# SwiGLU gate and up with the weights stationary and both parts of the tokens streaming, in a four-FFN decoder trunk

## The chip, the cores and the metric

The kernel runs on one core of one Trainium2 chip. The core has a matrix engine (TensorE, PE in the profile), a vector engine (VectorE, DVE), a scalar engine (ScalarE, ACT), a general engine (GpSimd, POOL) and a queue engine that issues DMAs (SyncE, SP). Work lives in SBUF, matmul results in PSUM, which has eight banks of 128 partitions x 512 fp32 columns. The metric is the device time of one execution in microseconds; the median of 3 runs of the kernel before is 1009.85 us (1009.16 to 1009.86).

## The reference, cut to what matters

256 tokens of 1024 channels pass through two layers. In each layer, an FFN, a mixer and another FFN are added to the residual x, so there are four FFNs:

```python
for layer in range(2):
    x = x + 0.5 * swiglu(rms_norm(x, norm_ffn1[layer]), w_ffn1_in[layer], w_ffn1_out[layer])
    x = x + mixer(rms_norm(x, norm_mix[layer]))      # layer 0: convolution and sparse attention, layer 1: stick-breaking
    x = x + 0.5 * swiglu(rms_norm(x, norm_ffn2[layer]), w_ffn2_in[layer], w_ffn2_out[layer])
return rms_norm(x, norm_final)

def swiglu(x, w_in, w_out):                          # w_in 1024 x 5632, w_out 2816 x 1024
    gate, up = jnp.split(x @ w_in, 2, axis=-1)
    return (jax.nn.silu(gate) * up) @ w_out
```

All of it is float32. The norm divides each token by its own root mean square; its gain is per channel.

## The kernel before, in words

Every large product is made of three matmuls on split operands. A weight block arrives by DMA in a raw tile of 1 MB (SP's queue, line 74), ScalarE copies it to a rounded high part `wh` (L84) and VectorE takes the difference as a low part `wl` (L85); activations are split likewise into XH and XL. `mm3` (L202 to L204) then adds high x high, high x low and low x high in one PSUM bank.

Before an FFN the residual x [tokens, channels] is turned to channels on partitions. For each half t of the tokens and half hf of the channels, four transposes on TensorE (L143) write one bank, and ScalarE (L156) and VectorE (L157) evacuate it in four steps as XH and XL, each step taking its turn on the same tile. The gain goes in there. The norm factor of a token is not known yet at that point; squares on ScalarE (L126) and two small steps on GpSimd (L130, L131) make it, and it is applied later.

Gate and up: the tokens are stationary (128 of them at a time) and the weights stream, 512 columns wide (256 of gate and 256 of up). A chunk of 256 channels takes 2 halves of tokens x 8 channel blocks x 3 matmuls, and there are 11 chunks. The result has tokens on partitions, so the norm factor is a scalar per partition: SiLU (L226) and the product (L228) take it along. For the output product the result must have channels on partitions, so `act_turn` turns it: two transposes on TensorE (L235), a copy on ScalarE (L239), a subtraction on VectorE (L240). The output product `out_mm` of a chunk is issued one chunk later, into four banks that stay open through the FFN. At the end the residual is updated (L300) tile by tile, and the next stage's transposes wait in a list that `flush` issues.

PSUM: two banks for gate and up (ps_gu), two for transposes (ps_tr), four for the output (ps_po). In the first chunk of an FFN t=0 goes first as a whole, so that the transposes of t=1 stand in its middle. In the others the halves alternate.

The order on each engine is made by a scheduler when the program is built, from the order in which instructions are written and their dependences; each engine then runs its own list in order and waits on semaphores. `begin` fixes the order of the first chunk by hand: it fetches x in four pieces and the first weights in eight pieces of 256 KB, runs nine matmuls on zeros while they arrive, and turns half of the channels at a time.

Of the kernel before, what the change touches and what calls it, by code (L numbers as in the profile page):

```python
# [8 lines left out]
F32 = mybir.dt.float32  # L9
# [7 lines left out]
P = 128  # L17
# [4 lines left out]
NCH = 11  # L22
# [24 lines left out]
def trunk_kernel(ctx: ExitStack, tc: tile.TileContext, a: dict):  # L47
# [46 lines left out]
    nc.sync.dma_start(gains, a["gains"])  # L94
# [5 lines left out]
    gfin = [None]  # L100
    XH = [None]
    XL = [None]
    RS = [None]

    def new_xt():
        XH[0] = acts.tile([P, ND, T], F32R, tag="XH", name="XH")
        XL[0] = acts.tile([P, ND, T], F32R, tag="XL", name="XL")
# [3 lines left out]
    half = const.tile([P, 1], F32, name="half")  # L111
    G.memset(half, -0.5)
# [15 lines left out]
    def rms(t):  # L128
        ms = small.tile([P, 1], F32, tag="ms", name="ms")
        G.tensor_scalar(ms, sq[t][:, 0:1], sq[t][:, 1:2], EPS, op0=ALU.add, op1=ALU.add)  # L130
        latest["pool"] = G.tensor_tensor(RS[0][:, t:t + 1], ms, half, op=ALU.pow)  # L131
# [8 lines left out]
    def turn_pe(src):  # L140
        pt = bank(ps_tr, "tr")
# [4 lines left out]
    def turn(t, hf, src, ni):  # L146

        pt = turn_pe(src)
        evacuate(pt, t, hf, ni, range(4))

    def evacuate(pt, t, hf, ni, ks):
        for k in ks:
            dt = hf * 4 + k
            g = gains[:, ni, dt:dt + 1]
            ts = slice(t * P, (t + 1) * P)
            latest["act"] = S.activation(XH[0][:, dt, ts], pt[:, k * P:(k + 1) * P], AF.Copy, scale=g)  # L156
            latest["dve"] = V.scalar_tensor_tensor(XL[0][:, dt, ts], pt[:, k * P:(k + 1) * P], g, f(XH[0][:, dt, ts]),  # L157
                                                   op0=ALU.mult, op1=ALU.subtract)
# [3 lines left out]
    def flush():  # L162
        for go in pending:
            go()
        pending.clear()

    def updated(t, hf, then):
# [5 lines left out]
        if kind == "ffn":  # L173
            pending.append(lambda: turn(t, hf, halves(t, hf), ni))
# [14 lines left out]
        if kind == "mix":  # L189
            for h in range(2):  # L190
                hs = slice(h * 512, (h + 1) * 512)
                V.tensor_scalar(o[:, hs], halves(t, h), r, None, op0=ALU.mult)
                pending.append(lambda h=h, hs=hs: turn(t, h, o[:, hs], ni))
# [18 lines left out]
    def ffn(w_in, w_out, then, first=None):  # L212
        xh, xl, rs = XH[0], XL[0], RS[0]
        po = {}
        hT = {}

        def gu_mm(pg, t, dt, w):
            (wh, wl), o = w[dt // 2], (dt % 2) * 512
            ts = slice(t * P, (t + 1) * P)
            mm3(pg, xh[:, dt, ts], xl[:, dt, ts], wh[:, o:o + 512], wl[:, o:o + 512], dt == 0, dt == ND - 1)  # L220

        hs = {}

        def act(t, pg):
            sg = small.tile([P, T], F32, tag="sg", name="sg", bufs=2)
            latest["silu"] = S.activation(sg, pg[:, :T], AF.Silu, scale=rs[:, t:t + 1])  # L226
            h = small.tile([P, T], F32, tag="h", name="h", bufs=2)
            V.scalar_tensor_tensor(h, pg[:, T:], rs[:, t:t + 1], sg, op0=ALU.mult, op1=ALU.mult)  # L228
            hs[t] = h

        def act_turn(c, t):
            h = hs[t]
            pt = bank(ps_tr, "tr")
            for k in range(2):
                PE.transpose(pt[:, k * P:(k + 1) * P], h[:, k * P:(k + 1) * P], ident)  # L235
            hh = small.tile([P, 2, P], F32R, tag="hh", name="hh", bufs=6)
            hl = small.tile([P, 2, P], F32R, tag="hl", name="hl", bufs=6)
            pv = pt[:, :T].rearrange("p (k q) -> p k q", k=2)
            S.activation(hh, pv, AF.Copy)  # L239
            V.tensor_tensor(hl, pv, f(hh), op=ALU.subtract)  # L240
            hT[c, t] = hh, hl

# [728 lines left out]
```

## Time and profile before

| | before |
|---|---|
| median of 3 runs | 1009.85 us |
| profiled execution | 1010.14 us |
| its span | 1008.4 us |
| PE busy | 992.9 us (98%), 5048 matmuls |
| PE weight loads busy | 825.3 us (82%) |
| DVE busy | 598.7 us (59%) |
| ACT busy | 542.2 us (54%) |
| DMA, mean share of 16 engines | 49% |
| HBM traffic | 175.9 MB, 174 GB/s |
| mean granted PE clock | 0.999 |

The span is that of the core's instructions; 1.7 us of the profiled execution lie around it. The profile names an instruction by its line in the kernel's file, its engine and its tiles (out <- in). Busy time of PE is the sum over time in which at least one matmul is in flight, so it says little about how closely they follow each other; the distance from start to start does.

### The profile page before, as it was taken

How to read it: one execution, taken by the hardware profiler on the slowest of the kernel's cores; microseconds unless marked ns; L12 is line 12 of the kernel's file. 1: busy time of each engine (PE TensorE's matmuls, PEld its weight loads, DVE VectorE, ACT ScalarE, POOL GpSimd, SP SyncE). 2: the span in 40 equal slices, each digit the busy share in tenths (PEclk: the TensorE clock that was granted, in tenths of full speed). 3: DMA queues.
4: the chain of work that ended last, by engine and by line, in shares of the span. 5: the costliest groups of instructions: out<-in, count | busy, mean ns of one | idle time of the engine just before them, and what ended most of it. 6: DMA issues, size and time to landing. Idle time of an engine off the chain costs nothing.

```text
span 1008.4 us, 13048 instructions
## 1 busy us (share of the span) xinstructions
PE 992.9 (98%) x5048; PEld 825.3 (82%) x5048; DVE 598.7 (59%) x891; ACT 542.2 (54%) x944; POOL 51.5 (5%) x97
## 2 busy tenths in 40 slices
PE   8999999999999999999999999999999999999997
PEld 6888888788888888888878888887898788888885
DVE  5655555599855655555575555546777575555553
ACT  7544444587545544444474444445887474444443
POOL 4000000132111000000000000000000010000001
PEclk9999999999999999999999999999999999999999
DMA  8745454454433654545445454553632255554521
GB/s 319 271 170 205 170 206 135 146 194 161 164 126 110 228 205 169 206 170 204 168 168 201 175 200 175 198 177 125 247 118 98 84 205 210 172 204 172 204 105 42
DMA packets 26702, 176.72 MB, mean 175 GB/s; under 512 B 3344, under 2 KB 3472, under 8 KB 5904
## 3 DMA queue, kind: packets, MB, share of 16 engines
q1 hardware_dynamic: 26640, 175.89, 49.1%
q8 instruction: 39, 0.64, 0.3%
q14 instruction: 23, 0.19, 0.1%
HBM read 174.83 MB, written 1.05 MB: 174 GB/s over the span
## 4 chain that ended last, share of the span: by engine, by line
PE 74%; issue 18%; DVE 3%; ACT 2%; POOL 1%; DMA 1%; SPq 0%; POOLq 0%; ACTq 0%
PE gu L203 11%; PE gu L202 11%; PE gu L204 11%; PE po L202 8%; PE po L203 8%; PE po L204 8%; PE gu L353 3%; PE gu L355 3%; PE gu L354 3%; PE tr L235 1%; PE tr L143 1%; ACT wh L84 1%; DVE wl L85 1%; DMA raw<-in_w_in 1%; PE po L787 1%
## 5 line engine op out<-in xcount | busy, mean ns | idle before, releaser
L85 DVE TENSOR_TENSOR wl<-raw,wh 128x1024 fp32r<-128x1024 f32 (+3 forms) x388 | 397.2, 1038 | 295.1 <-ACT wh L84 293.8
L84 ACT ACTIVATE wh<-raw 128x1024 fp32r<-128x1024 f32 (+3 forms) x396 | 349.3, 899 | 317.0 <-PE gu L204 169.3
L202 PE MATMUL gu<-wh,XH 128*128 128x512 f32 (+1 forms) x688 | 267.6, 389 | 1.4 <-ACT XH L156 1.3
L204 PE MATMUL gu<-wh,XL 128*128 128x512 f32 (+1 forms) x688 | 266.9, 388 | 0.1
L203 PE MATMUL gu<-wl,XH 128*128 128x512 f32 (+1 forms) x688 | 266.6, 387 | 0.0
L202 PEld LDWEIGHTS gu<-wh,XH 128*128 128x128 f32 x688 | 129.1, 188 | 29.7 <-ACT XH L156 3.8
L204 PEld LDWEIGHTS gu<-wh,XL 128*128 128x128 f32 x688 | 129.1, 188 | 26.8 <-DVE XL L157 0.6
L203 PEld LDWEIGHTS gu<-wl,XH 128*128 128x128 f32 x688 | 129.2, 188 | 26.6 <-DVE wl L85 0.4
L202 PE MATMUL po<-wh,hh 128*128 128x512 f32 x352 | 143.9, 409 | 0.0
L204 PE MATMUL po<-wh,hl 128*128 128x512 f32 x352 | 138.0, 392 | 0.0
L203 PE MATMUL po<-wl,hh 128*128 128x512 f32 x352 | 137.8, 392 | 0.0
L353 PE MATMUL gu<-XH,wh 128*128 128x256 f32 x288 | 83.7, 291 | 1.6 <-DVE u L476 1.2
L355 PE MATMUL gu<-XH,wl 128*128 128x256 f32 x288 | 81.4, 283 | 0.0
L354 PE MATMUL gu<-XL,wh 128*128 128x256 f32 x288 | 81.4, 283 | 0.0
L204 PEld LDWEIGHTS po<-wh,hl 128*128 128x128 f32 x352 | 66.1, 188 | 14.1
L203 PEld LDWEIGHTS po<-wl,hh 128*128 128x128 f32 x352 | 66.4, 189 | 11.5
L202 PEld LDWEIGHTS po<-wh,hh 128*128 128x128 f32 x352 | 66.2, 188 | 11.3
L226 ACT ACTIVATE sg<-gu,rs 128x256 f32<-128x256 f32 x80 | 38.0, 475 | 61.3 <-PE gu L204 61.2
L353 PEld LDWEIGHTS gu<-XH,wh 128*128 128x128 f32 x288 | 55.1, 191 | 2.0 <-issue 1.3
L228 DVE SCALAR_TENSOR_TENSOR h<-gu,rs,sg 128x256 f32<-128x256 f32 x80 | 38.7, 483 | 30.2 <-ACT sg L226 30.2
L354 PEld LDWEIGHTS gu<-XL,wh 128*128 128x128 f32 x288 | 55.1, 191 | 0.1
L355 PEld LDWEIGHTS gu<-XH,wl 128*128 128x128 f32 x288 | 55.0, 191 | 0.0
(207 smaller groups left out, 874.5 us busy)
## 6 DMA issues: line engine op xcount, KB each, us to landing
raw<-in_w_in SPq DMA_DIRECT2D x86, 1024.0 KB, 4.7
raw<-in_w_out SPq DMA_DIRECT2D x44, 1024.0 KB, 4.7
raw<-in_w_ab SPq DMA_DIRECT2D x10, 1024.0 KB, 4.8
raw<-in_w_qk SPq DMA_DIRECT2D x8, 1024.0 KB, 4.8
raw<-in_w_out_ab SPq DMA_DIRECT2D x4, 1024.0 KB, 4.7
raw<-in_w_v SPq DMA_DIRECT2D x4, 1024.0 KB, 4.7
raw<-in_w_out_sb SPq DMA_DIRECT2D x4, 1024.0 KB, 4.9
raw<-in_w_in SPq DMA_DIRECT2D x8, 256.0 KB, 6.3
```

Source lines behind the costliest of these rows:

```text
L84: S.activation(h[:, ms], r[:, ms], AF.Copy)
L85: eng.tensor_tensor(l[:, ms], r[:, ms], f(h[:, ms]), op=ALU.subtract)
L143: PE.transpose(pt[:, k * P:(k + 1) * P], src[:, k * P:(k + 1) * P], ident)
L202: PE.matmul(out, lh, rh, start=first, stop=False)
L203: PE.matmul(out, lh, rl, start=False, stop=False)
L204: PE.matmul(out, ll, rh, start=False, stop=last)
L226: latest["silu"] = S.activation(sg, pg[:, :T], AF.Silu, scale=rs[:, t:t + 1])
L228: V.scalar_tensor_tensor(h, pg[:, T:], rs[:, t:t + 1], sg, op0=ALU.mult, op1=ALU.mult)
L235: PE.transpose(pt[:, k * P:(k + 1) * P], h[:, k * P:(k + 1) * P], ident)
L353: PE.matmul(pq, wh[:, dt], XH[0][:, dt], start=dt == 0, stop=False)
L354: PE.matmul(pq, wh[:, dt], XL[0][:, dt], start=False, stop=False)
L355: PE.matmul(pq, wl[:, dt], XH[0][:, dt], start=False, stop=dt == ND - 1)
```

## The change

Gate and up are computed with the weights stationary: a block of 128 columns of gate or of up is loaded, and the tokens stream. XH and XL of all 256 tokens are now halves of one tile XX, so that one matmul streams [XH | XL], 512 columns (L260), against `wh`, and one streams XH, 256 columns (L261), against `wl`. Gate and up of a channel block c (22 of them, 128 channels each) fill the two banks of a pair: high products in the first 256 columns of a bank, with the low-weight products added to them, and the products with XL in the other 256.

The result has channels on partitions and needs no transposes, so `act_turn` and the pool ps_tr go. It has tokens along the free axis, so the norm factor has to lie along columns: `factor` scales the identity by it (L242), and a matmul with ones (L244) spreads it over all partitions; ScalarE copies that out (L245). For a block ScalarE copies the XL part (L273), VectorE adds the other (L274) and multiplies by the factor (L275), then come SiLU (L276), the product (L277) and the split (L278, L279). The output product of a block is issued two blocks later.

PSUM is now two pairs of banks and four output banks. Transposes and the mixers' projections take halves of a pair from `half`. `begin` issues a piece of x and the gains from ScalarE's queue, takes the weights of the first two blocks in pieces, and turns both token halves of a channel half into one pair. The residual's tiles are updated in another order where an FFN follows, and the flushes move with them.

```diff
     ps_gu = ctx.enter_context(tc.tile_pool(name="ps_gu", bufs=2, space=PSUM))
-    ps_tr = ctx.enter_context(tc.tile_pool(name="ps_tr", bufs=2, space=PSUM))
     ps_po = ctx.enter_context(tc.tile_pool(name="ps_po", bufs=4, space=PSUM))
+    spare = []
+    def pair(name="gu"):
+        return ps_gu.tile([P, 2, 512], F32, tag="gu", name=name)
+    def half():
+        if not spare:
+            both_ = pair("hb")
+            spare.extend((both_[:, 1], both_[:, 0]))
+        return spare.pop()
...
+    def parts(name):
+        xx = acts.tile([P, ND, 2, T], F32R, tag="XX", name=name)
+        return xx, xx[:, :, 0], xx[:, :, 1]
...
-    def flush():
+    def flush(get=half):
         for go in pending:
-            go()
+            go(get())
...
     def ffn(w_in, w_out, then, first=None):
...
+        def factor():
+            dg = small.tile([P, 2, T], F32, tag="gus", name="dg", bufs=1)[:, 0]
+            for t in range(NT):
+                V.tensor_scalar(dg[:, t * P:(t + 1) * P], ident, rs[:, t:t + 1], None, op0=ALU.mult)
+            pr = bank(ps_po, "po")[:, :T]
+            PE.matmul(pr, ones, dg, start=True, stop=True)
+            S.activation(RB, pr, AF.Copy)
...
+        def gu_mm(c, w, dts):
+            if c not in pgs:
+                pgs[c] = pair()
+            pg = pgs[c]
+            for dt in dts:
+                wh, wl = w[dt // 4]
+                for s in range(2):
+                    o = (dt % 4 * 2 + s) * P
+                    PE.matmul(pg[:, s], wh[:, o:o + P], xx[:, dt].rearrange("p a q -> p (a q)"), start=dt == 0, stop=False)
+                    PE.matmul(pg[:, s, :T], wl[:, o:o + P], xx[:, dt, 0], start=False, stop=dt == ND - 1)
+        def act(c, n=1):
...
+            for i in range(n):
+                ts = slice(i * T // n, (i + 1) * T // n)
+                tl = slice(T + i * T // n, T + (i + 1) * T // n)
+                S.activation(gu[:, :, ts], pg[:, :, tl], AF.Copy)
+                V.tensor_tensor(gu[:, :, ts], pg[:, :, ts], gu[:, :, ts], op=ALU.add)
+                V.tensor_tensor(gu[:, :, ts], gu[:, :, ts], RB[:, None, ts].to_broadcast([P, 2, T // n]), op=ALU.mult)
+                latest["silu"] = S.activation(sg[:, ts], gu[:, 0, ts], AF.Silu)
+                V.tensor_tensor(sg[:, ts], gu[:, 1, ts], sg[:, ts], op=ALU.mult)
+                S.activation(hh[:, ts], sg[:, ts], AF.Copy)
+                V.tensor_tensor(hl[:, ts], sg[:, ts], f(hh[:, ts]), op=ALU.subtract)
...
+        w = [weights(0), weights(1)]
+        gu_mm(0, w[0], range(4))
+        flush(lambda: bank(ps_po, "po"))
+        gu_mm(1, w[1], range(4))
+        gu_mm(0, w[0], range(4, ND))
+        factor()
+        act(0)
+        gu_mm(1, w[1], range(4, ND))
+        act(1)
+        for c in range(2, NF):
+            gu_mm(c, weights(c), range(ND))
+            act(c, NT if c == NF - 1 else 1)
+            if c % 2 == 0 and c < NF - 2:
+                wos[c // 2 - 1] = units(w_out[c // 2 - 1])
+            if c < NF - 2:
+                for t in range(NT):
+                    out_mm(c - 2, t)
...
+        order = [(0, 0), (1, 0), (0, 1), (1, 1)] if then[0] == "ffn" else [(0, 0), (0, 1), (1, 0), (1, 1)]
...
-        pq = bank(ps_gu, "gu")[:, :T]
+        pq = half()[:, :T]
...
+        get_x(0, 0, nc.sync)
+        get_x(1, 0, S)
+        S.dma_start(gains, a["gains"])
+        get_w(0, 0, 2)
+        get_w(1, 0, 1)
+        for t in range(NT):
+            get_x(t, 1, nc.sync)
+        get_w(0, 1, 2)
+        get_w(1, 1, 1)
...
             for hf in range(2):
-                pts = [turn_pe(halves(t, hf)) for t in range(NT)]
+                pts = pair()
```

On TensorE at the start, the kernel before has transposes of the second channel half (tr) amid the first chunk's gate and up (gu, two banks, one for each token half):

```order
L202 MATMUL gu_264<-wh_156,XH_102 128x512
L203 MATMUL gu_264<-wl_157,XH_102 128x512
L143 MATMUL tr_170<-ident_92,x_91 128x128 x4
L143 MATMUL tr_175<-ident_92,x_91 128x128 x4
L204 MATMUL gu_264<-wh_156,XL_103 128x512
L202 MATMUL gu_265<-wh_156,XH_102 128x512
```

and the kernel after has both channel halves' transposes ahead of them:

```order
L904 MATMUL po_115<-warm_93 128x512
L922 MATMUL gu_135<-ident_88,x_87 128x128 x8
L922 MATMUL gu_158<-ident_88,x_87 128x128 x8
L260 MATMUL gu_236<-XX_100,wh_124 128x512
L261 MATMUL gu_236<-XX_100,wl_125 128x256
L260 MATMUL gu_236<-XX_100,wh_124 128x512
```

The sixteen transposes of x now come before every gate and up matmul, and both kinds write tiles of the pool of pairs.

On TensorE at the crossing from the first mixer to the FFN behind it, the kernel before ends the out-projection (po), begins gate and up of t=0, and has the transposes of t=1 in their middle:

```order
L204 MATMUL gu_3224<-wh_3210,XL_3012 128x512
L202 MATMUL gu_3224<-wh_3210,XH_3011 128x512
L203 MATMUL gu_3224<-wl_3211,XH_3011 128x512
L204 MATMUL gu_3224<-wh_3210,XL_3012 128x512
L143 MATMUL tr_3238<-ident_92,x_91 128x128 x4
L143 MATMUL tr_3251<-ident_92,x_91 128x128 x4
L202 MATMUL gu_3224<-wh_3216,XH_3011 128x512
L203 MATMUL gu_3224<-wl_3217,XH_3011 128x512
```

and the kernel after ends the out-projection, turns the last two tiles (hb, a half of a pair, and po) and then begins gate and up:

```order
L220 MATMUL po_3219<-wh_3229,YY_2215 128x512
L221 MATMUL po_3219<-wl_3230,YY_2215 128x512
L222 MATMUL po_3219<-wh_3229,YY_2215 128x512
L160 MATMUL hb_3279<-ident_88,x_87 128x128 x4
L160 MATMUL po_3387<-ident_88,x_87 128x128 x4
L260 MATMUL gu_3370<-XX_3145,wh_3352 128x512
L261 MATMUL gu_3370<-XX_3145,wl_3353 128x256
```

The last transposes moved from amid the gate and up matmuls to ahead of them.

On ScalarE at that crossing, the kernel after has weight splits (L96) among the copies of turned tiles (L167, from hb_3279, which holds (0,0) and then (0,1), and hb_3317, which holds (1,0)) and the squares (L144):

```order
L96 ACTIVATE wh_3352<-raw_3350 128x1024
L167 ACTIVATE XX_3145<-hb_3279,gains_86 128x128
L96 ACTIVATE wh_3356<-raw_3350 128x1024
L167 ACTIVATE XX_3145<-hb_3317,gains_86 128x128
L96 ACTIVATE wh_3362<-raw_3360 128x1024
L167 ACTIVATE XX_3145<-hb_3279,gains_86 128x128
L96 ACTIVATE wh_3366<-raw_3360 128x1024
L167 ACTIVATE XX_3145<-hb_3317,gains_86 128x128
L96 ACTIVATE wh_3479<-raw_3477 128x1024
L167 ACTIVATE XX_3145<-hb_3279,gains_86 128x128
L167 ACTIVATE XX_3145<-hb_3317,gains_86 128x128
L144 ACTIVATE scr_3340,ssq_3305<-x_87 128x512
```

The copies of the tile in hb_3317 stand at every second place or further apart, with splits between.

## Rows read from the trace of the kernel before

**Rows 1.** Table of windows: busy time (x instructions) by engine, clock, DMA.
```profile
0.00:20.00 20.00, 17.07 (x72) 11.74 (x73) 8.79 (x25) 12.81 (x31) 9.87 (x30) 1.00 0.86 315
20.00:185.00 165.00, 165.00 (x750) 135.78 (x748) 92.63 (x106) 82.48 (x110) 1.99 (x4) 1.00 0.54 194
```

**Rows 2.** Timeline of PE inside an FFN: start, duration, line, tiles.
```profile
564.11 0.39 PE L204 MATMUL gu<-wh,XL 128*128 128x512 f32 x1
...
566.15 0.39 PE L204 MATMUL po<-wh,hl 128*128 128x512 f32 x1
566.38 0.38 PE L235 MATMUL tr<-ident,h 128*128 128x128 f32 x2
566.51 0.48 PE L202 MATMUL po<-wh,hh 128*128 128x512 f32 x1
566.83 0.39 PE L203 MATMUL po<-wl,hh 128*128 128x512 f32 x1
```

**Rows 3.** Groups by line, the transposes of the product: busy, mean ns.
```profile
L235 PE MATMUL tr<-ident,h 128*128 128x128 f32 x176 | 33.7, 273 | 0.2 <-DVE h L228 0.2
```

**Rows 4.** Timeline of PE in the stick-breaking mixer, a 256-column projection.
```profile
719.47 0.28 PE L354 MATMUL gu<-XL,wh 128*128 128x256 f32 x1
...
720.55 0.28 PE L354 MATMUL gu<-XL,wh 128*128 128x256 f32 x1
```

**Rows 5.** Page, costliest groups: weight loads of that projection.
```profile
L354 PEld LDWEIGHTS gu<-XL,wh 128*128 128x128 f32 x288 | 55.1, 191 | 0.1
```

**Rows 6.** Timeline of PE in the first mixer, fp32 matmul of 256 columns.
```profile
255.20 0.70 PE L675 MATMUL po<-pcT,VC 128*128 128x256 f32 x2
255.55 0.47 PE L353 MATMUL gu<-XH,wh 128*128 128x256 f32 x1
```

**Rows 7.** Timeline of PE at the start and at the second channel block.
```profile
7.04 0.47 PE L202 MATMUL gu<-wh,XH 128*128 128x512 f32 x1
...
9.69 0.76 PE L202 MATMUL gu<-wh,XH 128*128 128x512 f32 x2 [0.98 <-ACT XH L156]
...
20.42 0.39 PE L202 MATMUL po<-wh,XH 128*128 128x512 f32 x1
```

**Rows 8.** Timeline of SP's queue at the start: the last pieces of x.
```profile
4.06 0.91 SPq L859 DMA_DIRECT2D x<-in_x  x2
```

**Rows 9.** DMA issues by group: KB each, median us to landing.
```profile
raw<-in_w_in SPq DMA_DIRECT2D x8, 256.0 KB, 6.3
x<-in_x SPq DMA_DIRECT2D x4, 256.0 KB, 5.5
```

**Rows 10.** Groups by line and shape, VectorE and ScalarE.
```profile
L85 DVE TENSOR_TENSOR wl<-raw,wh 128x1024 fp32r<-128x1024 f32 x284 | 347.0, 1225 | 288.4 <-ACT wh L84 287.6
L84 ACT ACTIVATE wh<-raw 128x1024 fp32r<-128x1024 f32 x284 | 300.1, 1060 | 299.1 <-PE gu L204 168.2 <-PE po L204 115.9 <-PE gu L354 12.7
L300 DVE SCALAR_TENSOR_TENSOR x<-po,x 128x512 f32<-128x512 f32 x16 | 11.0, 687 | 11.9 <-PE po L204 11.8
L157 DVE SCALAR_TENSOR_TENSOR XL<-tr,gains,XH 128x128 fp32r<-128x128 f32 x96 | 30.0, 346 | 10.2 <-ACT XH L156 9.1
```

**Rows 11.** Timeline of ScalarE at the crossing from first mixer to FFN.
```profile
311.67 0.63 ACT L126 ACTIVATE scr<-x 128x512 bf16<-128x512 f32 x1 [2.80 <-DVE x L327]
312.42 0.63 ACT L126 ACTIVATE scr<-x 128x512 bf16<-128x512 f32 x1
...
316.25 0.60 ACT L156 ACTIVATE XH<-tr,gains 128x128 fp32r<-128x128 f32 x2
...
318.20 2.02 ACT L84 ACTIVATE wh<-raw 128x1024 fp32r<-128x1024 f32 x2
```

**Rows 12.** Timeline of PE at the same crossing.
```profile
319.38 0.39 PE L204 MATMUL po<-wh,YL 128*128 128x512 f32 x1
...
322.33 1.04 PE L143 MATMUL tr<-ident,x 128*128 128x128 f32 x8
323.13 0.47 PE L202 MATMUL gu<-wh,XH 128*128 128x512 f32 x1
```

More of the change, by code (lines that the diff above doesn't have):

```diff
@@ L21 @@
 ND = 8
-NCH = 11
+NF = 22
 U = 1024
@@ L231, in act_turn @@
[L231 to L241, printed above, removed]
@@ new lines, in weights @@
+        def weights(c):
+            if first and c < 2:
+                return first[c]
+            return units(w_in[c])
+        def gu_mm(c, w, dts):
[8 more added lines that the diff above has]
+                    PE.matmul(pg[:, s, :T], wl[:, o:o + P], xx[:, dt, 0], start=False, stop=dt == ND - 1)
@@ new lines, in ffn @@
+        if then == ("mix", 2):
+            switch("exp_and_others", latest["silu"])
+        for i in range(NF // 2 - 2, NF // 2):
+            wos[i] = units(w_out[i])
+        if then[0] != "end":
+            new_xt()
+        new_rs()
+        order = [(0, 0), (1, 0), (0, 1), (1, 1)] if then[0] == "ffn" else [(0, 0), (0, 1), (1, 0), (1, 1)]
+        for t, hf in order[:2]:
+            for c in range(NF - 4, NF - 1):
+                out_mm(c, t, (hf,))
+        for n, (t, hf) in enumerate(order):
+            for c in range(NF - 1 if n < 2 else NF - 4, NF):
+                out_mm(c, t, (hf,))
+                if c == NF - 3 and then[0] == "ffn":
+                    flush()
+            V.scalar_tensor_tensor(halves(t, hf), po[t, hf], 0.5, halves(t, hf), op0=ALU.mult, op1=ALU.add)
+            if n == 2 and then[0] != "ffn":
+                flush()
+            updated(t, hf, then)
@@ L343, in rest @@
                     self.mm(1, n, (hf,))
+                    if hf and n == 4:
+                        flush()
                 if hf == 0:
@@ L362, in more_constants @@
         V.tensor_copy(c["identb"], ident)
-        c["ones"] = const.tile([P, P], F32, name="ones")
-        G.memset(c["ones"], 1.0)
         z = small.tile([P, T], F32, tag="zz", name="zz", bufs=1)
@@ L445, in mixer0 @@
         for t in range(NT):
-            pv = bank(ps_gu, "gu")
+            pv = half()
             ts = slice(t * P, (t + 1) * P)
@@ L498, in mixer0 @@
             r = load(a["w1"][b])
-            po = bank(ps_tr, "tr")
+            po = half()
             for i in range(2):
@@ L517, in hidden @@
             hs = hss[b]
-            ph = bank(ps_tr, "tr")
+            ph = half()
             for m in range(2):
@@ L536, in comp_k @@
         def comp_k():
-            pc = bank(ps_tr, "tr")[:, :32]
+            pc = half()[:, :32]
             PE.matmul(pc, w2[:, 0:2].rearrange("p a d -> p (a d)"), gls[0].rearrange("p g c -> p (g c)"), start=True,
@@ L572, in comp_scores @@
         def comp_scores():
-            pcs = bank(ps_tr, "tr")
+            pcs = half()
             pcv = pcs.rearrange("p (n s c) -> p n s c", n=16, s=2)
@@ L595, in comp_turn @@
         def comp_turn():
-            pct = bank(ps_tr, "tr")
+            pct = half()
             for t in range(NT):
@@ L649, in turn_p @@
             p0, p1 = pr[j]
-            pt = bank(ps_tr, "tr")
+            pt = half()
             PE.transpose(pt[:, 0:P], p0[:, g, b], ident)
@@ L745, in mixer1 @@
             for t in range(NT):
-                pv = bank(ps_gu, "gu")
+                pv = half()
                 ts = slice(t * P, (t + 1) * P)
@@ L819, in values @@
             e = es[p]
-            py = bank(ps_tr, "tr")
+            py = half()
             for h in range(2):
```

186 lines of the change are left out of this document (63 added, 123 removed).

## The prediction

> **What bounds the kernel now.** I read the table of windows first, since shares over the whole span hide the stages. The reader is to see that inside a feed-forward network (FFN) TensorE is busy for 165.00 of 165.00 us while VectorE has 92.6 and ScalarE 82.5 [rows 1]: there the time is the number of matmuls times their pitch, and nothing that another engine saves counts. Busy time flatters TensorE, because its matmuls overlap, so I took pitches from the timeline, start to start. A 512-column matmul stands every 2.04 / 9 = 0.227 us (564.11 to 566.15) [rows 2], a 256-column one every 1.08 / 9 = 0.120 us [rows 4]. TensorE is idle only at the start, at the crossings between stages and at the end. So the change has two accounts: pitches in the streams, and waits at the crossings.
>
> **Streams: what goes.** The 88 pairs of transposes of the product (L235, 176 instructions [rows 3]) go. From 566.15 to 566.83 there are two 512-column matmuls and one pair: 0.68 - 2 x 0.227 = 0.227 us for a pair [rows 2], 88 x 0.227 = **-20.0 us**. By their own mean of 273 ns [rows 3] it would be 48 us, but that is latency which overlaps its neighbours.
>
> **Streams: what comes.** Gate and up took 11 x 2 x 8 x 3 = 528 matmuls of 512 columns per FFN, 119.7 us. They become 22 x 8 x 2 = 352 pairs of 512 and 256 columns: the same columns, but 352 x (0.227 + 0.120) = 122.0 us, since two narrow ones (0.240) take more than one wide one (0.227). With pitches unrounded that is 2.35 us, and for four FFNs **+9.4 us**. The order 512, 256, 512, 256 isn't in the trace; its bounds are the two pitches in it, 0.227 for the wide and between 0.113 (half) and 0.227 for the narrow, so 0 to +160 us; I take 0.120, because the mixer's row is of the same width and also loads weights for every matmul.
>
> The trace shows that a weight load of 191 ns [rows 5] stands behind a pitch of 120 ns [rows 4], so loads overlap each other and the matmuls. The Trainium skill, "TensorE: Matmul & The Clock Gate", section "Back-to-back issue gap", says that in a stream of loads and matmuls the spacing is set by both. By a strict reading, with a load as the floor of a narrow matmul, 4 x 352 x (0.191 - 0.120) = 100 us would be added; the mixer's row speaks against that reading, and it is a rival below.
>
> The norm factor now comes by one fp32 matmul of 128x256 per FFN. The mixer's fp32 pair of that width takes 255.20 to 255.55, 0.35 us [rows 6]: 4 x 0.35 = **+1.4 us** (2.8 if its 0.70 of duration is waited for).
>
> VectorE and ScalarE get more work per channel block: on VectorE three splits of 1.225, two passes of 512 at 0.69 and two of 256 at no more than that, under 6.5 us; on ScalarE three of 1.06, one of 512 at 0.63 and two narrower, under 5.1 us [rows 10, 11]. A block takes TensorE 8 x 2 x 0.347 + 12 x 0.227 = 8.3 us, so in the steady stream this is hidden. If the chain of a block came late in each of 80, at 0.3 us it would be 24 us; the two blocks between gate/up and its use leave 16 us for a chain of some 4, so I cost it at nothing.
>
> Streams together: -20.0 + 9.4 + 1.4 = -9.2 us.
>
> **Crossings: why they get worse.** In the old form a half of the tokens could begin gate/up while the other half was still being turned: 18 out-projection matmuls, then 12 of gate/up for t=0, with the transposes for t=1 only behind these (322.33) [rows 12]. Now a matmul streams both halves of the tokens, so nothing can begin before all four turned tiles have been evacuated far enough; and gate/up takes a pair of banks as one tile, of which there are two, and the turned tiles sit in the same two pairs. I followed each semaphore of the first matmuls in the changed order.
>
> The start. Before, gate/up runs from 7.04, with a gap to 9.69, and the second chunk of 256 channels begins at 20.42 [rows 7]. After, all 16 transposes stand ahead of the first gate/up matmul, so it needs the last piece of x. The last two pieces of x are issued from 4.06 to 4.97, the second at some 4.5 [rows 8], and pieces of 256 KB took a median of 5.5 to 6.3 us there [rows 9]; the same 2 MB come before it, hence some 10.8. Transposes and first evacuation: 11.5. Two channel blocks of 128, the equal of one old chunk: 2 x 5.55 = 11.1, hence 22.6. The third block needs the pair of the first. ScalarE reads that behind the factor's matmul (23.0) and its copy (23.4), 0.63 to 24.0; VectorE's add stands behind a split that ends at about 24.4, plus 0.69: 25.1. Against 20.42, and without the 0.35 counted above, that is 4.3. I take **+4.5** of 3 to 9; the upper end has a granted clock that falls in the pause (it is 1.00 in the first 20 us before [rows 1]).
>
> Mixer to FFN, twice. Let s be the start of the last out-projection matmul (319.38 in the first). The best possible gate/up start is s + 0.23 + 0.80 for eight transposes (322.33 to 323.13) [rows 12] = s + 1.0. In the changed order the first gate/up matmul writes the pair from which tile (1,0) was turned, and so waits for VectorE's fourth copy of that tile. The transposes of (0,0) begin at s - 17 x 0.227 - 0.8 = s - 4.65, and ScalarE's first copy at s - 4.15. From there to the fourth copy of (1,0), ScalarE has ten copies at 0.30 (two in 0.60), five weight splits at a pitch of 0.95 and two squares at 0.75 (311.67 to 312.42) [rows 11]: 3.0 + 4.75 + 1.5 = 9.25, to s + 5.1, and VectorE's 0.35 more [rows 10], s + 5.45: 4.4 late. The third block then waits for the first's pair: factor copy, read, one split and add, 0.4 + 0.63 + 1.2 + 0.69 plus a split on ScalarE, 0.95, less the 2.77 of the second block's last 16 matmuls: 1.1. That is 5.5; before loses something at the crossing too, so I take **+5.0** each, +10 (bounds +1 to +7 each, as the splits stand ahead or not).
>
> FFN to FFN, once: there the first wait is for the copies of (0,1) with the same splits between; I get gate/up at s + 4.65, 3.6 late, and 1.1 at the third block. Of these 4.7 I take **+4.0** (1 to 5).
>
> On banks the Trainium skill, "Perfetto Trace Analysis", section "Matmuls", says that independent groups of matmuls should rotate through different banks so that evacuation of one overlaps the next. No row of before can show what two pairs do here; by that rule the crossings must lose, which is the sign I have from the chains.
>
> Mixers: projections and turned tiles now share pairs, and the second half of a pair waits until the first has been read. I counted eight or nine such waits, each between 0 (other matmuls stand between) and 1.0 (a read of 0.69 and its start [rows 10]): 0 to 9, I take **+2.5**.
>
> **The sum.** 1010.14 - 9.2 + 4.5 + 10 + 4.0 + 2.5 = 1021.9 for the profiled execution; its span is 1008.4, and the 1.7 around it stay. The median of the runs is 0.3 below it: **1021.6 us**.
>
> **Rivals.**
> 1. The crossings are covered (20 in 100): splits land late or early enough that the copies overtake nothing, and each start loses 1 us or less. For it: VectorE and ScalarE are idle half the time. Against: the order on ScalarE is fixed, and it has five splits ahead of the copy that frees the bank. 1009.85 - 9.2 + 3 = 1003.6, faster.
> 2. The narrow matmul is bound by its weight load (4 in 100): +100, 1110. The mixer's pitch speaks against.
> 3. The new chain doesn't fit behind the stream (8 in 100): ScalarE's read of a pair waits in order behind a split which itself waits for TensorE, and each of 80 blocks loses 0.2 to 0.4: 16 to 32 more, 1038 to 1054. It decides once the chain of a block exceeds its 8.3 us. Rows of busy time give 6.5 at most.
> 4. The costs cancel (4 in 100): crossings of about 9 altogether, 1010.
>
> The forecast has 64 in 100, with a range of its own of 1013 to 1031. Faster by over 0.2% (which is about what a measurement of this kernel can tell from no change) is rival 1, 20; within it is rival 4, 4; slower is the rest, 76. The range that should hold 8 in 10 reaches from 1002, just under the point of rival 1, to 1034, between the forecast's own end and rival 3.
>
> **What would show it.** In the profile after: no L235; L260 and L261 at a pitch of 0.347 for the two; TensorE idle for about 4 us ahead of the first L260 at three crossings, released by VectorE L168, with five L96 among ScalarE's copies just before; a second gap of about 1 us ahead of the third block, released by VectorE L274; gate/up starting at 11 to 12 us instead of 7.04. I am wrong if TensorE's starts lie within 2 us of s at the crossings (then 1004), or if gaps repeat in each block inside the FFNs.

## The result, and the profile after

The changed kernel takes 1079.02 us (median of 4 runs, 1078.31 to 1079.82) against 1009.86 before: 1.069 times as long, 95% interval 1.067 to 1.071. It was forecast at 1021.6, with 1034 as the upper end, so the sign was right and the size far off: 69 us were lost where 12 were forecast.

The page of the changed kernel (busy time x instructions; TensorE's granted clock in tenths; groups by line) shows TensorE busier in total and yet idle for longer:

```profile
PE 1020.4 (95%) x5583; PEld 864.9 (80%) x5583; DVE 714.2 (66%) x1085; ACT 579.4 (54%) x1038; POOL 43.6 (4%) x93
PEclk9999999889999899999999999999999989999999
L260 PE MATMUL gu<-XX,wh 128*128 128x512 f32 x1408 | 508.6, 403 | 11.3 <-DVE XX L168 9.1
```

The transposes are gone, as they should be. The digits of 8 in the clock line are new: before, the clock stood at its upper level in the stretches of [rows 1]. To see where the time went I cut the span at the start of each stage's fourth residual update (VectorE L300, L327 before; L328, L355 after):

| stage | before, us | after, us | difference |
|---|---|---|---|
| first FFN, with the start | 196.6 | 203.8 | +7.2 |
| first mixer | 124.6 | 148.0 | +23.4 |
| second FFN | 187.1 | 193.7 | +6.6 |
| third FFN | 188.8 | 193.2 | +4.4 |
| second mixer | 119.4 | 139.1 | +19.7 |
| fourth FFN | 185.1 | 191.9 | +6.8 |
| end | 6.9 | 6.8 | -0.1 |

43 of the 68 us lie in the two mixers, whose arithmetic the change leaves alone. The table of windows has their engines (columns as in [rows 1]). The kernel before, its two mixers:

```profile
196.60:321.20 124.60, 120.69 (x870) 107.19 (x870) 95.04 (x198) 77.51 (x204) 25.20 (x42) 1.00 0.41 144
697.00:816.40 119.40, 119.12 (x771) 102.66 (x770) 80.62 (x168) 87.16 (x192) 2.30 (x4) 1.00 0.38 133
```

The changed kernel, the same two stages:

```profile
203.80:351.80 148.00, 131.00 (x867) 112.80 (x865) 95.58 (x198) 78.47 (x204) 22.94 (x42) 0.94 0.35 121
738.70:877.70 139.00, 125.98 (x768) 105.33 (x766) 81.01 (x169) 87.15 (x192) 2.06 (x4) 0.98 0.33 114
```

The reader is to see that VectorE and ScalarE do the same work (95.0 and 95.6, 77.5 and 78.5 us in the first mixer) while TensorE's idle time grows from 3.9 to 17.0 us and from 0.3 to 13.0, 25.8 us more in the two. It is also busy for 17.2 us more (131.0 against 120.7 and 126.0 against 119.1), at a granted clock of 0.94 and 0.98 in place of 1.00 (the clock is shown as a share of 2.4 GHz; 0.50 is its lower level). The clock explains some 9 of these 17.2 us: in the two mixers TensorE is busy for 20.2 us at the lower level, where its matmuls stand 0.21 us apart in place of 0.12 (shown below). What the other 8 are is open. What it waits for stands in the list of waits, here of the changed kernel's first mixer (total, times, longest):

```profile
PE hb L538 <- DVE u L504: 3.5, 1, 3.5
PE hb L383 <- DVE XX L168: 3.2, 1, 3.2
PE po L638 <- DVE q L591: 2.6, 2, 1.4
PE hb L222 <- DVE XX L168: 1.5, 1, 1.5
```

Three of the four are matmuls that write a half of a pair (hb). In the two mixers the list has 28 waits for VectorE or ScalarE, 27 us in all, of which 16, with 18.8 us, stand ahead of a matmul that writes a half; before it has 7, 3.8 us in all, the longest 1.2. The list alone doesn't tell a wait for a bank from a wait for data: L168 also writes XX, which L383 and L222 read. L538 and L383 read nothing that L504 and L797 write, so their waits are for the bank. One place in the second mixer shows the form. TensorE's timeline of the changed kernel:

```profile
787.20 0.40 PE L851 MATMUL hb<-e,V 128*64 128x128 f32 x4
790.42 0.38 PE L383 MATMUL hb<-XX,wh 128*128 128x256 f32 x1 [2.83 <-DVE qb L797]
...
790.88 0.28 PE L383 MATMUL hb<-XX,wh 128*128 128x256 f32 x1
...
791.60 0.28 PE L383 MATMUL hb<-XX,wh 128*128 128x256 f32 x1
...
792.11 0.41 PE L383 MATMUL hb<-XX,wh 128*128 128x256 f32 x1
...
792.75 0.41 PE L383 MATMUL hb<-XX,wh 128*128 128x256 f32 x1
```

VectorE's timeline of the same place:

```profile
788.15 0.42 DVE L797 SCALAR_TENSOR_TENSOR qb<-hb,qb 64x256 fp32r<-64x256 f32 x1 [0.57 <-ACT qb L796]
788.88 0.69 DVE L825 SCALAR_TENSOR_TENSOR sp<-po,e 128x512 f32<-128x512 f32 x1 [0.32 <-ACT e L823]
789.49 0.41 DVE L826 SCALAR_TENSOR_TENSOR sp<-po,e 128x256 f32<-128x256 f32 x1
789.94 0.43 DVE L797 SCALAR_TENSOR_TENSOR qb<-hb,qb 64x256 fp32r<-64x256 f32 x1
```

The projection that starts at 790.42 writes the second half of a pair. By its semaphore it waits for L797 at 789.94, which reads the first half. VectorE gets there late: between its two readings it has two steps of other work (L825, L826), the first of which itself waits for ScalarE. So 2.83 us pass. Then a second loss follows: the same projection's matmuls stand 0.12 us apart at first (790.88 to 791.60, six steps) and 0.21 us from 792 on (792.11 to 792.75, three steps). The table of windows has the clock there (third number from the end):

```profile
788.00:790.00 2.00, 0.00 (x0) 0.00 (x0) 1.50 (x4) 1.95 (x6) 0.00 (x0) 1.00 0.96 406
790.00:791.00 1.00, 0.58 (x4) 0.58 (x5) 0.94 (x3) 0.58 (x2) 0.00 (x0) 1.00 0.18 74
791.00:792.00 1.00, 1.00 (x10) 1.00 (x9) 1.00 (x2) 0.00 (x0) 0.00 (x0) 0.88 0.00 0
792.00:794.00 2.00, 2.00 (x11) 2.00 (x11) 1.29 (x4) 0.00 (x0) 0.00 (x0) 0.50 0.00 0
...
796.00:798.00 2.00, 2.00 (x17) 1.65 (x16) 0.57 (x2) 2.00 (x6) 0.00 (x0) 1.00 0.00 0
```

TensorE had been idle from 788 to 790; the clock was still 1.00 when it began again, then 0.88, then 0.50, the lower level of 1.2 GHz, and back at 1.00 by 796. So behind the pause TensorE works for a while at the lower level with work at hand.

### The profile page after: what moved, and what is told of

The parts are those of the page before. It is cut to its first block, busy times and chain, and to the rows that moved or that the text cites. A ratio compares the mean times of both kernels' runs of the same rounds, so it can differ in the third digit from the quotient of the medians.

```text
span 1076.5 us, 14431 instructions
## 1 busy us (share of the span) xinstructions
PE 1020.4 (95%) x5583; PEld 864.9 (80%) x5583; DVE 714.2 (66%) x1085; ACT 579.4 (54%) x1038; POOL 43.6 (4%) x93
## 4 chain that ended last, share of the span: by engine, by line
PE 49%; issue 18%; ACT 4%; DVE 4%; POOL 0%; POOLq 0%; ACTq 0%; DVEq 0%
PE gu L260 15%; PE gu L261 8%; PE po L220 5%; PE po L221 5%; PE po L222 5%; PE hb L383 2%; PE hb L384 2%; PE hb L385 2%; DVE wl L97 2%; ACT wh L96 1%; PE hb L220 1%; PE po L694 1%; PE po L813 1%; PE hb L221 1%; DVE XX L168 1%
## 5 line engine op out<-in xcount | busy, mean ns | idle before, releaser
L260 PE MATMUL gu<-XX,wh 128*128 128x512 f32 x1408 | 508.6, 403 | 11.3 <-DVE XX L168 9.1
L96 ACT ACTIVATE wh<-raw 128x1024 fp32r<-128x1024 f32 (+3 forms) x396 | 349.4, 895 | 297.0 <-PE gu L260 136.5
L261 PE MATMUL gu<-XX,wl 128*128 128x256 f32 x1408 | 398.2, 283 | 0.0
L260 PEld LDWEIGHTS gu<-XX,wh 128*128 128x128 f32 x1408 | 268.5, 191 | 78.0 <-DVE XX L168 9.8
L261 PEld LDWEIGHTS gu<-XX,wl 128*128 128x128 f32 x1408 | 269.9, 192 | 2.9
L222 PE MATMUL po<-wh,hl 128*128 128x512 f32 x352 | 137.1, 390 | 0.0
L278 ACT ACTIVATE hh<-sg 128x256 fp32r<-128x256 f32 (+1 forms) x92 | 37.5, 408 | 106.5 <-DVE sg L277 106.5
L383 PE MATMUL hb<-XX,wh 128*128 128x256 f32 x288 | 84.7, 295 | 7.7 <-DVE XX L168 3.2
L384 PE MATMUL hb<-XX,wh 128*128 128x256 f32 x288 | 82.8, 288 | 0.0
L385 PE MATMUL hb<-XX,wl 128*128 128x256 f32 x288 | 82.8, 288 | 0.0
L222 PEld LDWEIGHTS po<-wh,hl 128*128 128x128 f32 x352 | 66.1, 188 | 14.6
L383 PEld LDWEIGHTS hb<-XX,wh 128*128 128x128 f32 x288 | 56.4, 196 | 10.4 <-ACT gate L482 3.6
L279 DVE TENSOR_TENSOR hl<-sg,hh 128x256 fp32r<-128x256 f32 (+1 forms) x92 | 38.0, 413 | 40.0 <-ACT hh L278 39.8
L275 DVE TENSOR_TENSOR gus<-gus,rb 128x512 f32<-128x512 f32 (+1 forms) x92 | 61.6, 669 | 3.0
L274 DVE TENSOR_TENSOR gus<-gu,gus 128x512 f32<-128x512 f32 (+1 forms) x92 | 60.8, 661 | 1.0 <-ACT gus L273 0.8
L385 PEld LDWEIGHTS hb<-XX,wl 128*128 128x128 f32 x288 | 56.5, 196 | 0.0
L384 PEld LDWEIGHTS hb<-XX,wh 128*128 128x128 f32 x288 | 56.3, 196 | 0.2
```

Source lines behind the costliest of these rows:

```text
L96: S.activation(h[:, ms], r[:, ms], AF.Copy)
L222: PE.matmul(out, ll, rh, start=False, stop=last)
L260: PE.matmul(pg[:, s], wh[:, o:o + P], xx[:, dt].rearrange("p a q -> p (a q)"), start=dt == 0, stop=False)
L261: PE.matmul(pg[:, s, :T], wl[:, o:o + P], xx[:, dt, 0], start=False, stop=dt == ND - 1)
L274: V.tensor_tensor(gu[:, :, ts], pg[:, :, ts], gu[:, :, ts], op=ALU.add)
L275: V.tensor_tensor(gu[:, :, ts], gu[:, :, ts], RB[:, None, ts].to_broadcast([P, 2, T // n]), op=ALU.mult)
```

## The experiments

**Four single banks.** In the changed kernel, the pairs alone are undone; a block's read and add become two instructions each.

```diff
-    ps_gu = ctx.enter_context(tc.tile_pool(name="ps_gu", bufs=2, space=PSUM))
+    ps_gu = ctx.enter_context(tc.tile_pool(name="ps_gu", bufs=4, space=PSUM))
     def pair(name="gu"):
-        return ps_gu.tile([P, 2, 512], F32, tag="gu", name=name)
+        return [bank(ps_gu, "gu") for _ in range(2)]
     def half():
-        if not spare:
-            both_ = pair("hb")
-            spare.extend((both_[:, 1], both_[:, 0]))
-        return spare.pop()
+        return bank(ps_gu, "gu")
...
-                S.activation(gu[:, :, ts], pg[:, :, tl], AF.Copy)
-                V.tensor_tensor(gu[:, :, ts], pg[:, :, ts], gu[:, :, ts], op=ALU.add)
+                for s in range(2):
+                    S.activation(gu[:, s, ts], pg[s][:, tl], AF.Copy)
+                    V.tensor_tensor(gu[:, s, ts], pg[s][:, ts], gu[:, s, ts], op=ALU.add)
```

> The changed kernel, with its two pairs of PSUM banks undone into four single banks: gate and up take two tiles, projections and turned tiles one each, and a block's read and add become two instructions of 256 columns each. Everything else as in the change. In the changed kernel the stage of the first mixer is 148.0 us long against 124.6 before, that of the second 139.1 against 119.4: 43 of the 68 us lost. Theory A (the pair is one tile: a half waits until the other half has been read, TensorE idles, and its clock then falls): the mixers come back to within 4 us of 124.6 and 119.4, the first gate and up matmul no longer waits for a turned pair, and the whole is 1025 to 1040. Theory B (the mixers are slower because the scheduler put splits and mixer work in another order; the pairs are incidental): the mixers stay above 140 and 132, the whole is 1070 to 1085. Theory C (half and half): about 1050.

Measured: 1023.54 us (1.0141 times before, 95% interval 1.0126 to 1.0156). That is 55.5 us off the change and 1.5 below theory A's range. The mixers take 125.3 and 120.1 us, 0.7 each over before. Its longest wait in the first mixer, from the list of waits:

```profile
PE gu L381 <- DVE kd L519: 1.1, 1, 1.1
```

Both its mixers in the table of windows:

```profile
202.50:327.80 125.30, 120.44 (x871) 106.67 (x869) 95.54 (x201) 78.07 (x206) 24.92 (x42) 1.00 0.42 144
706.90:827.00 120.10, 118.77 (x772) 102.00 (x770) 81.47 (x172) 87.78 (x194) 2.32 (x4) 1.00 0.38 132
```

The granted clock is 1.00 in both mixers again. The two mixers have 8 waits in place of 28, 4.2 us in all. The later FFNs come down as well, from +6.6, +4.4, +6.8 to +2.5, +0.8 and +2.2 over before: at the first crossing gate and up begins 0.23 us behind the last out-projection matmul (325.89 to 326.12), and no longer waits for a turned pair. Theory A stands against theory B as far as the pairs are the cause. But the order of instructions is not kept apart from them: with single banks the scheduler also puts TensorE's matmuls into another order, in the first mixer nearly that of before.

**The pairs alone, in the kernel before.** The reverse of it: before, with its four banks for gate, up and transposes made into two pairs, and nothing else.

```diff
-    ps_tr = ctx.enter_context(tc.tile_pool(name="ps_tr", bufs=2, space=PSUM))
+    def pair(name="gu"):
+        return ps_gu.tile([P, 2, 512], F32, tag="gu", name=name)
+    def half():
+        if not spare:
+            both_ = pair("hb")
+            spare.extend((both_[:, 1], both_[:, 0]))
+        return spare.pop()
...
-            pg = [bank(ps_po, "po") if c == 1 else bank(ps_gu, "gu") for _ in range(NT)]
+            if c == 1:
+                pg = [bank(ps_po, "po") for _ in range(NT)]
+            else:
+                both = pair()
+                pg = [both[:, t] for t in range(NT)]
...
-        pq = bank(ps_gu, "gu")[:, :T]
+        pq = half()[:, :T]
```

> The kernel before with one thing of the change added: its two banks for gate and up and its two for transposes become two pairs of banks, each pair one tile; a chunk's two token halves take the halves of a pair, and projections, turned tiles and turned products take halves one after the other. No other part of the change. Theory (the pair alone makes the mixers wait): the mixers take 140 to 150 and 132 to 142 us against 124.6 and 119.4; the FFNs may lose as well, since turned products share pairs with gate and up; the whole is 1040 or more. Rival (the mixers were slowed by the change's other order, the pairs only let it show): the mixers stay within 4 us of before.

Measured: 1084.26 us (1.0739, 1.0723 to 1.0756), the mixers at 160.1 and 136.0. The longest waits of its first mixer:

```profile
PE hb L524 <- DVE kd L507: 4.8, 2, 4.5
PE hb L153 <- DVE XL L167: 3.2, 1, 3.2
PE hb L212 <- ACT gate L468: 3.2, 1, 3.2
```

With nothing else of the change, the pairs cost as much as the whole change. The first mixer lost more than expected (160 against an upper end of 150). With the experiment above, the pairs are shown to be the cause from both sides. Here too the scheduler's order moves with the pairs: compared matmul by matmul, about 65 in 100 of TensorE's instructions in the first mixer stand in the order of before, where single banks in the changed kernel have 97 in 100. So the two runs price the binding of banks with the order that follows from it; how much is the waiting alone is not shown. The Trainium skill, "Perfetto Trace Analysis", section "Matmuls", says that independent groups should rotate through different banks, so that the evacuation of one overlaps the next. In pairs the groups do stand in different banks, and the overlap is lost all the same, with 1079.0 against 1023.5 and 1084.3 against 1009.6 us: here it took separate tiles too.

**Zeros in the pause at three crossings.** 14 matmuls on zeros ahead of gate and up in the later FFNs of the changed kernel.

```diff
+        if not first:
+            idle = bank(ps_po, "po")
+            for i in range(14):
+                PE.matmul(idle, warm[:, :P], warm, start=True, stop=True)
         gu_mm(0, w[0], range(4))
```

> The changed kernel with 14 matmuls on zeros (128 columns stationary, 512 moving, bf16, 3.2 us in all) ahead of gate and up in each of the three later FFNs. They fill the pause in which TensorE waits for turned tiles and compute nothing that is used. In the changed kernel the granted clock falls to the lower level in that pause and stays there for 6.8, 3.4 and 6.8 us. Theory A (a good part of what a crossing costs beyond its wait is the clock): the clock stays up at the three crossings, each FFN's start gets 1.5 to 3 us faster, the whole is 1070 to 1075. Rival (the clock costs nothing, since the weights arrive no faster): within 1.5 us of 1079, or slower by what the filling delays.

Measured: 1075.16 us (four runs, 1072.09 to 1076.97), 3.9 less than the change and just above theory A's upper end. In the profiles the second and fourth FFN get 2.5 and 2.3 us shorter, the third 0.4 longer; the mixers, which the zeros leave alone, differ by -1.6 and +1.1 between the same two profiles, so single stages are known no better than that. TensorE's timeline of the changed kernel at the first of these crossings, which answers to [rows 12]:

```profile
350.61 0.39 PE L222 MATMUL po<-wh,YY 128*128 128x512 f32 x1
351.94 0.66 PE L160 MATMUL hb<-ident,x 128*128 128x128 f32 x4 [0.95 <-DVE XX L168]
...
356.32 0.79 PE L260 MATMUL gu<-XX,wh 128*128 128x512 f32 x1 [3.12 <-DVE XX L168]
...
357.12 0.63 PE L260 MATMUL gu<-XX,wh 128*128 128x512 f32 x1
...
357.76 0.63 PE L260 MATMUL gu<-XX,wh 128*128 128x512 f32 x1
```

Its table of windows there:

```profile
354.00:356.00 2.00, 0.00 (x0) 0.00 (x0) 2.00 (x6) 2.00 (x7) 1.17 (x2) 0.71 0.74 307
356.00:358.00 2.00, 1.68 (x5) 1.49 (x6) 1.87 (x8) 1.66 (x5) 0.56 (x1) 0.50 0.60 135
```

With zeros, gate and up begins here at 353.50, 5.72 us behind the last out-projection matmul (347.78), and the clock stays; the table of windows of that run:

```profile
354.00:356.00 2.00, 2.00 (x13) 1.72 (x13) 2.00 (x5) 0.96 (x3) 0.00 (x0) 1.00 0.74 266
```

The start of gate and up is 5.71 us behind the last out-projection matmul in the change (350.61 to 356.32); I had worked out 5.45. So the wait was forecast to within 0.3 us, and what was left out is the clock behind it: 0.50 in the window from 356 to 358, where gate and up runs at a pair each 0.64 us (357.12 to 357.76) and not 0.353. At two of three crossings the theory holds. At the third, ahead of the third FFN, the clock stays up too, but gate and up begins 6.75 us behind the last out-projection matmul (539.55 to 546.30) where the change has 4.89 (544.84 to 549.73): the last transposes stand behind the zeros (543.40) and the factor's matmul ahead of gate and up (544.64), and the later start took back what the clock gave.

**Wide, wide, narrow, narrow.** The changed kernel with another order in each group of four.

```diff
-                for s in range(2):
-                    o = (dt % 4 * 2 + s) * P
-                    PE.matmul(pg[:, s], wh[:, o:o + P], xx[:, dt].rearrange("p a q -> p (a q)"), start=dt == 0, stop=False)
-                    PE.matmul(pg[:, s, :T], wl[:, o:o + P], xx[:, dt, 0], start=False, stop=dt == ND - 1)
+                os = [(dt % 4 * 2 + s) * P for s in range(2)]
+                for s, o in enumerate(os):
+                    PE.matmul(pg[:, s], wh[:, o:o + P], xx[:, dt].rearrange("p a q -> p (a q)"), start=dt == 0, stop=False)
+                for s, o in enumerate(os):
+                    PE.matmul(pg[:, s, :T], wl[:, o:o + P], xx[:, dt, 0], start=False, stop=dt == ND - 1)
```

> The changed kernel with each group of four gate and up matmuls in another order: the two of 512 columns first, then the two of 256 (changed: 512, 256, 512, 256). In the changed kernel a pair of wide and narrow takes 0.353 us in the steady stream, not the 0.347 of the forecast, and the matmuls behind it are slow for a while too, so a block of 128 channels takes 8.387 us where 8.267 was forecast and 8.410 is what before takes. Theory A (alternating widths cost it, because a weight load stands behind a narrow matmul that is too short to hide it): two wide ones hide more, or two narrow ones in a row hide less; the block's period moves by 0.05 us or more either way, 4 us or more in the whole. Rival (a fixed cost of each narrow matmul, wherever it stands): the period stays within 0.02 us of 8.387, the whole within 2 us.

Measured: 1070.36 us, 8.7 less. The period of a block is read in TensorE's timeline between two first matmuls of gate and up (the answer to [rows 2]). The changed kernel:

```profile
604.76 0.39 PE L260 MATMUL gu<-XX,wh 128*128 128x512 f32 x1
...
605.45 0.40 PE L260 MATMUL gu<-XX,wh 128*128 128x512 f32 x1
605.69 0.28 PE L261 MATMUL gu<-XX,wl 128*128 128x256 f32 x1
605.81 0.40 PE L260 MATMUL gu<-XX,wh 128*128 128x512 f32 x1
...
610.40 0.40 PE L220 MATMUL po<-wh,hh 128*128 128x512 f32 x1
...
613.15 0.39 PE L260 MATMUL gu<-XX,wh 128*128 128x512 f32 x1
```

This one:

```profile
608.13 0.62 PE L260 MATMUL gu<-XX,wh 128*128 128x512 f32 x2
...
616.42 0.39 PE L260 MATMUL gu<-XX,wh 128*128 128x512 f32 x1
```

8.39 and 8.29 us (8.387 and 8.293 over 68 blocks); before has 16.82 us for two, 8.410 for one. The order of widths alone is worth 0.094 a block, 8.3 us for 88 blocks. That the period moves with the order is shown; the reason that the theory gives for it, the weight load behind a narrow matmul, is not.

**Groups of four, and the two gains together.** Single banks with groups of two, and single banks with groups of four (two input blocks' wide matmuls, then their narrow ones).

```diff
+            for d0 in dts[::2]:
+                group = [(dt, s) + tuple(w[dt // 4]) + ((dt % 4 * 2 + s) * P,) for dt in (d0, d0 + 1) for s in range(2)]
+                for dt, s, wh, wl, o in group:
+                    PE.matmul(pg[s], wh[:, o:o + P], ...
+                for dt, s, wh, wl, o in group:
+                    PE.matmul(pg[s][:, :T], wl[:, o:o + P], ...
```

> The changed kernel with four single banks in place of two pairs (the first experiment, 1023.5 us, mixers at 125.3 and 120.1) and with the order wide, wide, narrow, narrow (the third, 8.7 us less than the change). Theory (the two costs are apart: waits on pairs in mixers and at crossings, pitch in the stream): they add, 1014 to 1016, with a block's period of 8.29. Rival (the third gained by shorter pauses, which are gone here): 1019 or more.

> As the run beside it, four single banks, with gate and up in groups of four wide matmuls and four narrow ones (two channel blocks of the input together). If each change of width costs something, halving their number again takes the block's period from 8.29 to about 8.25, 3 us in the whole. If it is a run of narrow ones that costs (in the mixer a row of narrow ones has a pitch of 0.120, in the groups of two 0.115), the period goes up instead, to 8.30 or more.

Measured: 1015.56 us (1.0063, 1.0047 to 1.0078) in groups of two: the gains add, 8.0 us on top of the single banks. In groups of four 1019.92 us (1.0104, 1.0089 to 1.0119), with a period of 8.353. So it is not the number of changes of width that counts: one, two and four in a row give 8.387, 8.293 and 8.353. In fours the narrow ones stand 0.118 apart (600.39 to 600.86 for four) and the twelve output matmuls behind them take 2.77 (603.66 to 606.43); in twos, in the run above, it is 0.115 (608.58 to 608.81 for two) and 2.73 (613.69 to 616.42). Why is open.

**The start.** On single banks and groups of two: the first 16 gate and up matmuls are issued ahead of the transposes of the second channel half, and the second block writes two output banks.

```diff
-                pgs[c] = pair()
+                pgs[c] = [bank(ps_po, "po") for _ in range(2)] if c == 1 else pair()
...
             for hf in range(2):
                 pts = pair()
...
+                if hf == 0:
+                    pg = pair()
+                    mm_block(pg, XX[0], w[0], range(4))
                 part(1, hf, 0, 1)
```

> The run with single banks and groups of two, with the start taken apart: the 16 gate and up matmuls on the first half of the channels stand ahead of the transposes of the second half, and the second channel block writes two output banks, so that the third finds the first's banks. In the change the third block begins at 27.5 us where before has its equal at 20.4. Theory (the start loses by waiting for the last piece of x, then for the first block's banks): gate and up begins at about 8, the third block at 22 to 23, the first FFN gets 4 to 5 us shorter than in the run without this, the whole is 1010 to 1011. Rival (DMA arrival of the weights sets the start): less than 1.5 us gained.

Measured: 1009.27 us (1.0002, 0.9993 to 1.0012): as fast as before. In the changed kernel TensorE's timeline of the start, which answers to [rows 7], reads:

```profile
10.14 0.48 PE L922 MATMUL gu<-ident,x 128*128 128x128 f32 x1 [3.60 <-DMA x<-in_x]
10.84 1.76 PE L922 MATMUL gu<-ident,x 128*128 128x128 f32 x7 [0.23 <-DMA x<-in_x]
12.25 0.78 PE L260 MATMUL gu<-XX,wh 128*128 128x512 f32 x1
...
24.65 0.70 PE L244 MATMUL po<-dg,ones 128*128 128x256 f32 x2 [0.46 <-DVE dg L242]
...
27.52 0.79 PE L260 MATMUL gu<-XX,wh 128*128 128x512 f32 x1 [2.17 <-DVE gus L274]
```

It had waited for the last piece of x until 10.84, for the factor, and 2.17 us for VectorE's add of the first block; the third block began at 27.52, where I had 25.1. In the experiment gate and up begins at 7.90 (7.04 before) and the third block at 22.89, both as the theory has them, but the first matmuls run at the lower level of the clock, which reads 0.52 from 7 to 14 us; TensorE's timeline of this run:

```profile
7.90 1.22 PE L232 MATMUL gu<-XX,wh 128*128 128x512 f32 x2 [2.60 <-DVE XX L165]
...
9.34 1.05 PE L232 MATMUL gu<-XX,wh 128*128 128x512 f32 x2
...
10.62 1.05 PE L232 MATMUL gu<-XX,wh 128*128 128x512 f32 x2
```

The first FFN is 2.6 us shorter in the profiles (200.1 against 202.7), less than the theory's 4 to 5; the later FFNs, in which the second block now writes output banks too, are 2.5 shorter together. The median gains 6.3. The profiled execution took 1012.24 us at a mean clock of 0.994, where eight of the ten have 0.997 or 0.998, so most of them had the low clock for less time than this trace shows.

**Zeros in the pause of that start.**

```diff
+                    with tc.issue_after(last.ins):
+                        for i in range(12):
+                            PE.matmul(idle, warm[:, :P], warm, start=True, stop=True)
                     pg = pair()
```

> The run with the rebuilt start (single banks, groups of two, first gate and up ahead of the second half's transposes: 1009.3 us, equal to before), with 12 matmuls on zeros behind the first eight transposes. In that run TensorE pauses from 5.3 to 7.9 us, and the granted clock is at the lower level from 7.3 to 14.1 us, while 16 gate and up matmuls and eight transposes run at half pace. The zeros fill the pause. Theory: the clock stays at the upper level, gate and up runs at 0.69 us for four from its start, the first FFN is 2.5 to 3.5 us shorter, the whole 1006 to 1007, faster than both kernels. Rival (the weights' arrival and the splits pace the start, not the clock): within 1 us of 1009.3.

TensorE's timeline of this run at the start:

```profile
6.00 2.75 PE L937 MATMUL po<-warm 128*128 128x512 bf16 x12
8.40 0.82 PE L232 MATMUL gu<-XX,wh 128*128 128x512 f32 x2
...
9.30 0.63 PE L232 MATMUL gu<-XX,wh 128*128 128x512 f32 x2
...
10.00 0.63 PE L232 MATMUL gu<-XX,wh 128*128 128x512 f32 x2
```

Measured: 1007.71 us (0.9986, 0.9977 to 0.9995 of before). Gate and up begins later, at 8.40, but four matmuls take 0.70 us from 9.30 on, where they took 1.28 (9.34 to 10.62). The first FFN comes to 197.1 us, 3.0 less in the profiles. The median gains 1.6, half of what was expected and between the ranges of theory and rival: the 3.0 is measured against the trace of 1012.24 us, which has more of the low clock than most executions of that kernel. This is the only version that beats before, by 0.14%.

## Why the prediction was wrong, step by step

- **Mixers, +2.5 with bounds 0 to 9: the step that failed.** It measured +43.1. I had found that a second half waits for the first's reading, counted eight or nine such places, and priced each by the read itself, at 1.0 us at most. But the reader stands in VectorE's or ScalarE's queue behind other work: single waits were 3.5, 3.2 and 2.8 us, there were 28 in place of 7, and behind the longer ones the clock fell: 25.8 us of idle time and 17.2 of longer busy time, some 9 of it the clock, make up the 43. Not every wait is one that I had counted: 12 of the 28 stand ahead of matmuls that write output banks, mostly for data that came late. In this kernel a wait's price was the place of its releaser in its own queue. I had followed those queues at the FFN crossings and not here.
- **Streams, -9.2.** A block of 128 channels takes 8.387 us where 8.410 was before, so 88 blocks save 2.0 us and not 10.6 ahead of the factor. The transposes' 20 us did go. The term that was off is the added one: the pair of wide and narrow takes 0.353 and not 0.347, which is 0.09 a block, and the twelve output matmuls take 2.75 (610.40 to 613.15) and not 2.72, 0.03 more; and the block before took 8.410 where 37 pitches of 0.2267 are 8.387. In the pair it is not the narrow matmul, for which I had taken the mixer's 0.120, that was off: from 400 to 480 us it stands 0.117 ahead of the next start. The wide one stands 0.236 ahead of the narrow one, where 0.227 was taken from a stream of wide ones (605.45 to 605.69 to 605.81 shows one pair). Rival 2, a full weight load for each narrow matmul, fell: that would be a pitch of 0.42 for a pair. Rival 3, a gap in each block, fell too: 68 blocks have the same period of 8.39.
- **Crossings and start, +18.5.** The FFNs lost 25.0 us in all; without the streams' -2.0 and the factor's 1.4, which is the forecast's and wasn't measured apart, that is some 25.6. The first waits were right: gate and up began 5.71, 4.89 and 5.74 us behind the last out-projection matmul where 5.45, 4.65 and 5.45 were worked out, released by VectorE's L168 as named. The start's third block came at 27.5 against 25.1. The second gap, 1.1 ahead of the third block, stood only at the start, with 2.17; at the three crossings there is none. Left out was the clock behind the waits, which I had allowed for in the upper bound at the start only: at the crossings 8, 5 and 8 pairs took 5.29, 3.25 and 5.20 us, some 6.3 more than at 0.353 each. So a gap that didn't come and a clock that wasn't counted partly cancel, and that the crossings came out as near as they did is in part luck.
- **Bounds and rivals.** The upper end of 1034 was too low because the mixers' bound held one term per wait. The sign was forecast from the crossings and the start, and these did lose more than the streams gained; so the reason for the sign was sound, but it was not the main cause. With single banks, where the crossings' waits are mostly gone, the kernel is still slower than before (1023.5), 5.9 us of it in the first FFN with the start. Rival 1 can't be had from banks alone: it takes single banks, the other order of widths, another start and zeros to get under before.

## What to carry to other kernels

When two independent results are put into one tile, whoever writes one can come to wait for the readers of the other, as in this kernel: look at every user of the pool, not only at the stage that the change is about. Price a new wait by where its releaser stands in its engine's queue, and add the matmuls that run at the lower clock behind a pause. A saving on TensorE is worth what the new pattern's own pitch leaves of it: here 20 us of transposes bought 2 us, and some 10 (88 x 0.117) once the order of widths was changed.

## What the runs showed that I had not expected

- The period of a block depends on the order of its matmuls, with TensorE waiting for no other engine: 8.387, 8.293 and 8.353 us for the same 32 and 12 matmuls.
- In one place the granted clock fell only after TensorE had begun again: 0.00 us busy from 788 to 790 at 1.00, then 0.88 and 0.50 with TensorE fully busy. In another it fell inside the pause: 0.00 us busy from 354 to 356 at 0.71. Matmuls on zeros, which compute nothing, won 3.9 us at the crossings and 1.6 at the start by keeping it at 2.4 GHz.
